# Causal masks and their identity as fp32r in two tables, instead of bf16 in one

## The chip, the cores and the metric

The kernel runs on one core of one Trainium2 chip. The metric is the device time of one launch in microseconds, the median of three runs.

## The reference, cut to what matters

One layer of a decoder: 1024 prompt tokens and 8 decode sequences of 8 tokens, width 1024. One input projection feeds two groups of heads, four differential heads and eight heads of native sparse attention (NSA; two groups of four with shared keys). Their outputs are joined and go through an output projection and a squared-ReLU MLP. Every score that a query must not see is set to -1e9 ahead of the softmax:

```python
def masked_softmax(s, mask):
    s = jnp.where(mask, s.astype(jnp.float32), NEG)
    m = jnp.max(s, axis=-1, keepdims=True)
    p = jnp.where(mask, jnp.exp(s - m), 0.0)
    return p / jnp.maximum(jnp.sum(p, axis=-1, keepdims=True), 1e-30)
# differential heads: kpos[None, :] <= tpos[:, None]
# NSA, compressed keys: cmp_end[None, :] <= tpos[:, None]; its window of 512 has a far edge too
```

The decode tokens attend in the same way to paged caches of 512 past tokens and to the 8 new ones.

## The kernel before, in words

The queries of the prompt are worked off in eight tiles of 128 tokens. Scores are built in PSUM banks of 128x512: two fp32r passes for the two halves of split query values (L404), and then, where a tile crosses the causal diagonal, one more matmul that adds a 128x128 mask of 0 and -1e9 (L411). It has an identity as its weights (`identb`) and the mask (`m_diag`) as its moving data, both bf16. The far edge of the window is added the same way (L408, `m_far`), the compressed branch starts its bank with a mask of 128x256 (L431, `m_cmp`), and the decode scores add masks of 8 columns (L1092 and L1172 `m_new`, L1173 `m_win`). VectorE then reduces the row maximum (L412) and ScalarE takes the exponential (L421).

The masks are loaded by `consts_b` at the start: pieces of the constant `c_mask` come by ScalarE's DMA queue into `raw` tiles and VectorE copies them into `maskb` (L213, L214).

The order of the stages: the projections and keys of NSA; `stage_nsa`, in which the queries of the prompt go through the compressed, selected and window branches (values L496, weights `pt`, values `vst` and `vcp`; the sums of a group are stored to `mixT` at L543); and then `stage_diff`, which works off the differential heads with the decode attention of both kinds beside them. Each decode batch of NSA (`dec_nsa`) loads four cache pages (L1143) and the window state (L1146), each of 128x4x256 fp32 in all, into tiles `kvp` of a pool of five, stores the shifted window back (L1148, L1149), transposes the keys (L1152), scores them (L1167, L1170 and the masks), and, when POOL has scaled the probabilities (L1186, `dpP`), transposes these (L1192). The projection of the differential heads (L331) stands behind that on TensorE. The differential pages are loaded at L1055 and transposed at L1058.

What sets the order: each engine runs its instructions strictly in the order of its own list, and so does each DMA queue (SP issues most of them). The lists come from the framework, which orders the instructions by a simulated schedule. Tiles are allotted from pools that lie one behind the other in SBUF: `xa`, `b`, `sg`, `sm`, then `bn`, which lives until the end of NSA, and then the pools of the stage. When a pool is left, the pools of the next stage take its bytes, and the first instruction that writes a tile waits for the last one that read what lay there:

```python
self.bn = e1(self.pool("bn"))
...
self.kvd = e2(self.pool("kvd", KVB))
...
self.dec_nsa_loads()
self.stage_diff()
```

Of the kernel before, what the change touches and what calls it, by code (L numbers as in the profile page):

```python
# [26 lines left out]
P = 128  # L27
# [3 lines left out]
NT = SEQ // P  # L31
# [15 lines left out]
# schedule  # L47
LAG = 5                  # token tiles by which the first keys / values trail the compression rows
REST = 7                 # items of those left over that go before the compression
QS = 1                   # first query tiles that use a score bank  # L50
KVB = 5                  # page buffers of the decode attention
NSU = (2, 2, 2, 2, 0)    # NSA decode batches around each change of heads
WDN = 10                 # weight buffers of the differential heads
WD = (1, 0, 1)           # per stage: low parts of the weights on VectorE (else GpSimd)
PS_N = (4, 2, 1, 1)      # PSUM banks of scores, transposes, outputs, products: NSA
PS_D = (3, 2, 1, 2)      # the same, differential heads
# [6 lines left out]
def merge(*lists):  # L63
    """emit several lists of (cost, thunk) interleaved in proportion to their total cost"""
# [20 lines left out]
def interleave(*lists):  # L85
    """the items of several lists in the order in which merge would run them"""
    out = []
    merge(*[[(c, lambda i=i: out.append(i)) for i in l for c in [i[0]]] for l in lists])
    return out


class Fill:
    """queue of background work; marks give the point that has to be reached before a given job"""
# [12 lines left out]
    def take(self, budget, key=None):  # L106
        """items up to the mark at least, then up to the budget"""
        need = self.marks.get(key, 0)
        out = []
        c = 0.0  # L110
        while self.pos < len(self.q) and (self.pos < need or c < budget):
            out.append(self.q[self.pos])
            c += self.q[self.pos][0]
            self.pos += 1
        return out
# [5 lines left out]
class Kern:  # L121
# [9 lines left out]
    # ---------------------------------------------------------------- helpers  # L131
# [3 lines left out]
    def evac(self, out, in_, n, scale=None):  # L135
        """PSUM -> SBUF copy on the less loaded of ScalarE and VectorE"""
# [59 lines left out]
    # ---------------------------------------------------------------- setup  # L196
# [7 lines left out]
    def consts_b(self, b):  # L204
        nc, A = self.nc, self.A
        self.identb = b.tile([P, P], BF, name="identb")
        nc.vector.tensor_copy(self.identb, self.ident)
        nm = A["c_mask"].shape[1]
        self.maskb = b.tile([P, nm], BF, name="maskb")
        for c in range(0, nm, 256):  # L210
            n = min(256, nm - c)
            mt = self.rawp.tile([P, 256], F32, name="raw")
            nc.scalar.dma_start(mt[:, :n], A["c_mask"][:, c:c + n])  # L213
            nc.vector.tensor_copy(self.maskb[:, c:c + n], mt[:, :n])  # L214
        self.m_diag = self.maskb[:, 0:128]
        self.m_far = self.maskb[:, 128:256]
        self.m_cmp = self.maskb[:, 256:768].rearrange("p (t n) -> p t n", t=NT)
        self.m_new = self.maskb[:, 768:776]
        self.m_win = self.maskb[:, 776:784]
# [30 lines left out]
    # ---------------------------------------------------------------- phase A: x -> normalised, transposed, split  # L250
    def phase_x(self, px):
        """load a token tile; transpose, split it and take its sum of squares. The weights carry the gain, the
        projections are scaled by 1 / rms on their way out of PSUM"""
# [26 lines left out]
    def gain_cols(self):  # L280
        """g_pre_mix as columns: [128, k]"""
# [7 lines left out]
    # ---------------------------------------------------------------- projections  # L289
    def load_w(self, src, n):  # L290
        """src(k) -> DRAM AP [128, ...] of n columns for contraction block k"""
# [28 lines left out]
    def proj(self, ps, ws, n, t, step=24):  # L320
        """thunks of step products each"""
# [18 lines left out]
    def rope(self, v, t, h):  # L340
        """v: SBUF AP [m, h, 64], rotated in place"""
# [14 lines left out]
    def dup(self, v):  # L356
        """[128, h, 64] -> tile [128, h, 2, 64] with each row block twice"""
# [5 lines left out]
    def k_stack(self, rd, kst, t, T=None):  # L363
        """two doubled sources [128 tok, 128] -> kst[half] [128, 2, 512]; partitions 0-63 hi, 64-127 lo"""
# [10 lines left out]
    def q_stack(self, rd, n, T=None):  # L375
        """n doubled sources [128 tok, 128] -> (hi, lo) stacks [128, n, 128], scaled by 1/8"""
# [10 lines left out]
    # ---------------------------------------------------------------- attention, prompt  # L387
# [3 lines left out]
    def scores(self, qs, j, kst, kc, i, kb0, sums, far):  # L391
        """exp(s - max) for key blocks kb0..i; returns the tile (absolute key columns); sums: [128, 2], one partial
        row sum per 512 keys"""
# [32 lines left out]
    def nsa_cmp_scores(self, g, i, st):  # L426
        """probabilities of the compressed branch, four heads, times gate / sum"""
# [24 lines left out]
    def nsa_scores(self, g, i, pr, st):  # L452
        """thunks: probabilities of heads 2 pr, 2 pr + 1 in the selected and window branches"""
# [30 lines left out]
    def nsa_values(self, g, i, pr, st):  # L484
        """thunks: weighted sums of the values for heads 2 pr, 2 pr + 1, all branches, into st['o']"""
# [64 lines left out]
    def diff_norm(self, od, rows, h, col0):  # L550
        """od: [rows, 128] head output (SBUF) -> sub-layer norm, transpose, store to mixT"""
# [73 lines left out]
    # ---------------------------------------------------------------- compression  # L625
    def unit_cmp(self):
        """projection of the compression branch's k, v rows: one list of thunks per token tile"""
# [32 lines left out]
    def compress_load(self, hb):  # L660
        """thunks: the cached compression rows (keys and values) of four batches, four pages each"""
# [1043 lines left out]
```

## Time and profile before

| | |
|---|---|
| time, median of 3 runs | 1871.66 us (1869.86 to 1874.77) |
| span of the profiled execution | 1873.6 us |
| TensorE busy (PE), weight loads (PEld) | 1783.9 us (95%), 1566.2 us (84%) |
| VectorE, ScalarE, GpSimd | 961.5 us, 720.6 us, 530.2 us |
| L411 masks, PE and PEld | 44.6 us and 18.7 us, 192 each |
| mean granted TensorE clock | 0.976 |

The profiled execution is one more than the three timed ones; its span is 1.9 us above their median and inside their spread, and the profile shows nothing around it. Matmuls are pipelined: the duration of one overlaps with its neighbours, and the time that it takes up is read from the distance of the starts.

### The profile page before, as it was taken

Reading aid. Unit: us, or ns where it says so; the run is one execution under the profiler, and the core shown is the slowest. Engines: PE = TensorE matmul, PEld = TensorE weight load, DVE = VectorE, ACT = ScalarE, POOL = GpSimd, SP = SyncE. Lnnn points to the kernel's source line nnn. Section 1 sums busy time; section 2 is a strip of 40 time slices with the busy share of each in tenths; the row PEclk is TensorE's granted clock in tenths of the full one; section 3 lists DMA queues with packets and bytes.
Section 4 is the critical chain, followed back from the end, with each engine's and each line's share of the span. In section 5 each row is a group of like instructions: output and inputs, shape, how many; then the busy total and the mean of one; then the engine's idle time right before and its main releaser. Section 6 shows DMA issues by size and latency. Waiting matters only on the chain. (4 is left out here: it accounts for less than half of the span.)

```text
span 1873.6 us, 31247 instructions
## 1 busy us (share of the span) xinstructions
PE 1783.9 (95%) x11379; PEld 1566.2 (84%) x11379; DVE 961.5 (51%) x2519; ACT 720.6 (38%) x1987; POOL 530.2 (28%) x749
## 2 busy tenths in 40 slices
PE   6788999999999999999979999999999999999996
PEld 6777776676657788778868799999999999999996
DVE  4357767667754666666564553333333333333336
ACT  4254446556652455555463342222222222222212
POOL 1133325333321111111151023333333333333313
PEclk8899899999999999999989999999999999999998
DMA  8531000022102524324263331111111111111104
GB/s 169 119 86 44 17 12 21 6 80 52 28 8 58 155 72 125 100 66 124 68 201 106 124 119 46 43 43 45 42 45 45 46 46 46 45 46 46 46 1 169
DMA packets 186533, 129.38 MB, mean 69 GB/s; under 512 B 30115, under 2 KB 177419, under 8 KB 186379
## 3 DMA queue, kind: packets, MB, share of 16 engines
q1 hardware_dynamic: 185082, 125.11, 23.5%
q10 hardware_dynamic: 1296, 2.27, 0.5%
q8 instruction: 90, 1.47, 0.3%
q14 instruction: 65, 0.52, 0.1%
HBM read 102.56 MB, written 24.78 MB: 68 GB/s over the span
## 5 line engine op out<-in xcount | busy, mean ns | idle before, releaser
L1355 PE MATMUL Dn<-h,w 128*128 128x384 f32 (+1 forms) x2304 | 388.6, 327 | 2.1 <-DVE w L1401 2.1
L1335 PE MATMUL U<-xt,w 128*128 128x384 f32 (+1 forms) x2304 | 388.5, 326 | 0.2 <-ACT xt L133 0.2
L1355 PEld LDWEIGHTS Dn<-h,w 128*128 128x128 f32 x2304 | 381.8, 188 | 2.3 <-ACT w L1395 2.3
L1335 PEld LDWEIGHTS U<-xt,w 128*128 128x128 f32 x2304 | 380.4, 188 | 0.6 <-ACT xt L133 0.4
L331 PE MATMUL M<-w,xt 128*128 128x384 f32 (+4 forms) x1584 | 294.6, 331 | 13.5 <-ACT nat L133 13.2
L1361 DVE TENSOR_TENSOR acc<-Dn,acc 128x384 f32<-128x384 f32 (+1 forms) x360 | 191.8, 535 | 204.9 <-PE Dn L1355 203.5
L331 PEld LDWEIGHTS M<-w,xt 128*128 128x128 f32 (+1 forms) x1584 | 245.1, 191 | 28.9 <-ACT nat L133 14.7
L162 POOL TENSOR_TENSOR w<-raw,w 128x512 fp32r<-128x512 f32 x128 | 170.8, 1346 | 177.4 <-ACT w L133 177.4
L421 ACT ACTIVATE p<-S,nm 128x512 f32<-128x512 f32 (+3 forms) x288 | 160.1, 562 | 103.6 <-DVE nm L416 57.1
L133 ACT ACTIVATE w<-raw 128x512 fp32r<-128x512 f32 (+1 forms) x160 | 96.6, 609 | 241.8 <-PE U L1335 166.0
L1343 DVE TENSOR_TENSOR h<-r,h 128x384 fp32r<-128x384 f32 (+1 forms) x96 | 52.0, 542 | 261.8 <-POOL r L1342 261.8
L412 DVE TENSOR_REDUCE nm<-S 128x1 f32<-128x512 f32 (+3 forms) x288 | 148.0, 527 | 58.1 <-PE S L411 37.0
L1339 ACT ACTIVATE r<-U 128x384 f32<-128x384 f32 (+1 forms) x96 | 45.4, 473 | 342.3 <-PE U L1335 342.3
L404 PE MATMUL S<-kst,qs 128*128 128x512 f32 (+3 forms) x576 | 163.2, 376 | 9.0 <-ACT p L421 7.9
L1342 POOL TENSOR_TENSOR r<-r 128x384 f32<-128x384 f32 (+1 forms) x96 | 77.3, 805 | 328.6 <-ACT h L1341 328.6
L475 POOL TENSOR_SCALAR p<-p,coef 128x640 f32<-128x640 f32 (+7 forms) x128 | 92.8, 738 | 146.4 <-DVE coef L472 79.6
L404 PEld LDWEIGHTS S<-kst,qs 128*128 128x128 f32 x576 | 94.5, 196 | 21.7 <-ACT p L421 11.1
L169 POOL TENSOR_TENSOR rs_r<-rs_t,mhalf 128x1 f32<-128x1 f32 (+1 forms) x63 | 36.3, 577 | 249.1 <-DVE rs_t L167 236.0
L1267 PE MATMUL C<-w,mh 128*128 128x512 f32 (+1 forms) x432 | 105.5, 401 | 0.8 <-DVE ctmp L1282 0.8
L351 POOL TENSOR_TENSOR rope<-nat,sin 128x128 f32<-128x128 f32 (+3 forms) x81 | 36.3, 448 | 245.5 <-ACT nat L133 234.4
L1267 PEld LDWEIGHTS C<-w,mh 128*128 128x128 f32 (+1 forms) x432 | 78.4, 184 | 22.3 <-DVE ctmp L1282 1.1
L511 PEld LDWEIGHTS T<-ident,p 128*128 128x128 f32 x528 | 57.1, 141 | 39.3 <-issue 35.6
(265 smaller groups left out, 2395.1 us busy)
## 6 DMA issues: line engine op xcount, KB each, us to landing
kvp<-cache_diff_kv SPq DMA_DIRECT2D x128, 128.0 KB
raw<-w_up SPq DMA_DIRECT2D x64, 256.0 KB
raw<-w_down SPq DMA_DIRECT2D x64, 256.0 KB
raw<-w_in SPq DMA_DIRECT2D x32, 192.0 KB
raw<-w_in SPq DMA_DIRECT2D x40, 128.0 KB
xin<-x_prompt SPq DMA_DIRECT2D x8, 512.0 KB
cst<-cache_nsa_kv SPq DMA_DIRECT2D x32, 128.0 KB
kvp<-cache_nsa_kv SPq DMA_DIRECT2D x32, 128.0 KB
```

The lines of the kernel that those rows point to most:

```text
L133: self.nc.scalar.activation(out, in_, AF.Copy, scale=scale)
L162: (nc.vector if self.lo_dve else nc.gpsimd).tensor_sub(lo, raw, f32(hi))
L331: nc.tensor.matmul(ps[1][:m, :n], self.xt[c][:, a, k, c0:c0 + m], ws[k][:, b, :n], start=i == 0, stop=i == len(ops) - 1)
L404: nc.tensor.matmul(S[:, a * P - lo:b * P - lo], qs[:, ps, j, :], kst[hf][:, kc, a * P - lo:b * P - lo], start=ps == 0, stop=ps == 1 and no ...
L412: nc.vector.reduce_max(nm[:, n:n + 1], S[:, a * P - lo:b * P - lo], axis=AX.X, negate=True)
L421: nc.scalar.activation(p[:, a * P:b * P], tiles[n][:, a * P - lo:b * P - lo], AF.Exp, bias=nm[:, 0:1], accum_out=sums[:, n:n + 1])
L475: nc.gpsimd.tensor_scalar(v, v, coef[:, sw + 1, j:j + 1], 0.0, op0=OP.mult, op1=OP.add)
L1267: nc.tensor.matmul(ps[:m], mhs[t][:, a, k, :m], ws[n][k][:, b], start=cnt == 0, stop=cnt == 3 * KC - 1)
L1335: nc.tensor.matmul(U[:, :n], ups[f][k // 4][:, a, k % 4, :], self.xt[c][:, b, k, :], start=cnt == 0, stop=cnt == 3 * KC - 1)
L1342: nc.gpsimd.tensor_mul(r[:, :n], r[:, :n], r[:, :n])
L1355: nc.tensor.matmul(O_[:, :n], dns[dm // 2][:, a, f, (dm % 2) * P:(dm % 2 + 1) * P], hs[f][:, b, :n], start=cnt == 0, stop=cnt == 5)
L1361: nc.vector.tensor_add(acc[c][:, dm], O_[:, :n], acc[c][:, dm])
```

## The change

The identity and the masks become fp32r. The one table of 784 columns in pool `b` is split in two: 144 columns (`m_diag`, `m_new`, `m_win`) stay in `b`, and 640 columns (`m_far`, `m_cmp`) go to `masks` in pool `bn`, which is given back at the end of NSA. The table is loaded in five pieces instead of four, so there is one DMA, one `raw` tile and one copy more. Pool `b` shrinks by 736 bytes per partition, and `bn` grows by 2560. (The rest of the change drops comments.)

```diff
--- before.py
+++ after.py
@@ consts_b
-        self.identb = b.tile([P, P], BF, name="identb")
+        self.identb = b.tile([P, P], FR, name="identb")
         nc.vector.tensor_copy(self.identb, self.ident)
-        nm = A["c_mask"].shape[1]
-        self.maskb = b.tile([P, nm], BF, name="maskb")
-        for c in range(0, nm, 256):
-            n = min(256, nm - c)
+        far = self.bn.tile([P, 640], FR, name="masks")
+        self.maskb = b.tile([P, 144], FR, name="maskb")
+        for c, n, dst in ((0, 128, self.maskb[:, 0:128]), (768, 16, self.maskb[:, 128:144]), (128, 256, far[:, 0:256]),
+                          (384, 256, far[:, 256:512]), (640, 128, far[:, 512:640])):
             mt = self.rawp.tile([P, 256], F32, name="raw")
             nc.scalar.dma_start(mt[:, :n], A["c_mask"][:, c:c + n])
-            nc.vector.tensor_copy(self.maskb[:, c:c + n], mt[:, :n])
+            nc.vector.tensor_copy(dst, mt[:, :n])
         self.m_diag = self.maskb[:, 0:128]
-        self.m_far = self.maskb[:, 128:256]
-        self.m_cmp = self.maskb[:, 256:768].rearrange("p (t n) -> p t n", t=NT)
-        self.m_new = self.maskb[:, 768:776]
-        self.m_win = self.maskb[:, 776:784]
+        self.m_far = far[:, 0:128]
+        self.m_cmp = far[:, 128:640].rearrange("p (t n) -> p t n", t=NT)
+        self.m_new = self.maskb[:, 128:136]
+        self.m_win = self.maskb[:, 136:144]
```

In the list of TensorE all separate weight loads of the bf16 identity go: 192 at L411, 32 at L408, 16 at L431 and 8 each at L1092, L1172 and L1173, 264 in all; the fp32r matmul loads its weights itself, as those of L404 do. The matmuls stay 10580. In the changed list the mask matmuls of L411 and L408 stand right ahead of an L331 in 46 places, of an L404 of 256 columns or more in 57 and of 128 columns in 13, of an L496 in 41, and of a transpose or another fp32 matmul in 67.

In the differential stage the page buffers `kvp` begin 736 bytes lower (170464 in place of 171200), and in the NSA stage the values of the second group, `vst`, end 1824 bytes higher (172064 in place of 170240). So the first page buffer now lies on `vst`.

SP's list at the change from NSA to the differential heads, before: the first pages (`cache_nsa_kv`) and the window states stand among the stores of `mixT`, in front of 13 loads of `w_in`, and the loads wait (in brackets, a counter of the DMA queue or of an engine) for PE alone.

```order
L543 DMA mixT<-pt 64x4x128 [waits DMAHW3_49,DVE_49]
L1143 ISA
L1143 DMA kvp<-cache_nsa_kv 128x256 [waits DMAHW4_49,PE_49]
L1143 ISA
L1143 DMA kvp<-cache_nsa_kv 128x256 [waits DMAHW5_49]
L1143 ISA
L1143 DMA kvp<-cache_nsa_kv 128x256 [waits DMAHW6_49]
L1143 ISA
L1143 DMA kvp<-cache_nsa_kv 128x256 [waits DMAHW7_49]
L1146 DMA kvp<-state_nsa_win_kv 128x4x256 [waits DMAHW0_49,PE_49]
```

The same loads in the changed kernel:

```order
L960 DMA o_diff_s<-nat 128x1x128 [waits DMAHW3_49,DVE_49,Activation_49]
L1143 ISA
L1143 DMA kvp<-cache_nsa_kv 128x256 [waits DMAHW4_49,PE_49,Pool_49]
L1143 ISA
L1143 DMA kvp<-cache_nsa_kv 128x256 [waits DMAHW5_49]
L1143 ISA
L1143 DMA kvp<-cache_nsa_kv 128x256 [waits DMAHW6_49]
L1143 ISA
L1143 DMA kvp<-cache_nsa_kv 128x256 [waits DMAHW7_49]
L543 DMA mixT<-pt 64x4x128 [waits DMAHW0_49,DVE_49]
L1146 DMA kvp<-state_nsa_win_kv 128x4x256 [waits DMAHW1_49]
```

They now stand behind the loads of `w_in`, behind the store of `o_diff_s` and behind all stores of `mixT` but the last, and the PE instruction for which the first page waits is the last L496 on `vst` of the NSA stage. The last store of `mixT`, which is the fold of the second group, stands between the pages and the window.

TensorE's list at the same place, before: the last values of NSA, the transposes of the first batch's pages and window and its first scores.

```order
L496 MATMUL o<-pt,vst 64x256 [waits Activation_49]
L496 MATMUL o<-pt,vcp_1467 64x256 [waits DVE_49]
L1152 MATMUL T<-ident,kvp 128x128 [waits DMAHW4_49,PE_49]
L1152 MATMUL T<-ident,kvp 128x128 [waits DMAHW5_49]
L1152 MATMUL T<-ident,kvp 128x128 [waits DMAHW6_49]
L1152 MATMUL T<-ident,kvp 128x128 [waits DMAHW7_49]
L1152 MATMUL T<-ident,kvp 128x128 [waits DMAHW0_49,PE_49]
L1152 MATMUL T<-ident,kvp 128x128 x3
L1167 MATMUL S<-kt,qndec 64x260 [waits Activation_49]
```

The same place in the changed kernel:

```order
L496 MATMUL o<-pt,vst 64x256 [waits Activation_49]
L496 MATMUL o<-pt,vcp_1471 64x256 [waits DVE_49]
L1152 MATMUL T<-ident,kvp 128x128 [waits DMAHW4_49,PE_49]
L1152 MATMUL T<-ident,kvp 128x128 [waits DMAHW5_49]
L1152 MATMUL T<-ident,kvp 128x128 [waits DMAHW6_49]
L1152 MATMUL T<-ident,kvp 128x128 [waits DMAHW7_49]
L1167 MATMUL S<-kt,qndec 64x260 [waits Activation_49]
L1167 MATMUL S<-kt,qndec 64x260 [waits DVE_49]
L1152 MATMUL T<-ident,kvp 128x128 [waits DMAHW1_49]
L1152 MATMUL T<-ident,kvp 128x128 x3
```

The end of the values and the first transposes stand next to each other in both. In the changed list the load of the pages is released by the last L496 on `vst`, and between it and the transposes that read these pages only the product on `vcp` is left. Behind these rows the window of the first batch, the pages and then the window of the second follow, then L1192, and only then the first L331 of the projection.

## Rows read from the trace of the kernel before

**Rows 1.** The page: span, then busy time of each engine.

```profile
span 1873.6 us, 31247 instructions
PE 1783.9 (95%) x11379; PEld 1566.2 (84%) x11379; DVE 961.5 (51%) x2519; ACT 720.6 (38%) x1987; POOL 530.2 (28%) x749
```

**Rows 2.** All mask instructions of L411: min/median/max ns, first and last start.

```profile
L411 PEld LDWEIGHTS <-identb x192: 95/96/146, 178.9 to 970.3; 128*128 128x128 bf16 x192
L411 PE MATMUL S<-maskb,identb x192: 218/230/330, 178.9 to 970.3; 128*128 128x128 bf16 x192
```

**Rows 3.** Groups by line: busy us, mean ns, idle before, releasers.

```profile
L404 PEld LDWEIGHTS S<-kst,qs 128*128 128x128 f32 x576 | 94.5, 196 | 21.7 <-ACT p L421 11.1 <-issue 4.7 <-ACT qs L133 2.2
```

**Rows 4.** Timeline of PE, four places: start us, us, instruction.

```profile
72.31 3.00 PE L331 MATMUL M<-w,xt 128*128 128x256 f32 x24
75.15 0.38 PE L370 MATMUL T<-ident,rd 128*128 128x128 f32 x2
...
228.21 0.23 PE L411 MATMUL S<-maskb,identb 128*128 128x128 bf16 x1
228.25 0.84 PE L331 MATMUL M<-w,xt 128*128 128x256 f32 x5
228.93 0.34 PE L404 MATMUL S<-kst,qs 128*128 128x384 f32 x1
...
330.35 0.23 PE L411 MATMUL S<-maskb,identb 128*128 128x128 bf16 x1
330.42 0.50 PE L511 MATMUL T<-ident,p 128*128 128x128 f32 x3
...
448.36 0.23 PE L411 MATMUL S<-maskb,identb 128*128 128x128 bf16 x1
448.40 0.71 PE L404 MATMUL S<-kst,qs 128*128 128x512 f32 x2
448.95 0.23 PE L411 MATMUL S<-maskb,identb 128*128 128x128 bf16 x1
```

**Rows 5.** Timeline of the start: the last copy of a mask on VectorE.

```profile
27.21 0.17 DVE L214 CAST maskb<-raw 128x16 bf16<-128x16 f32 x1 [3.09 <-DMA raw<-c_mask]
```

**Rows 6.** Timeline of SP in NSA: the first page loads.

```profile
381.87 2.35 SPq L1143 DMA_DIRECT2D kvp<-cache_nsa_kv  x4
...
384.91 1.93 SPq L1143 DMA_DIRECT2D kvp<-cache_nsa_kv  x4
```

**Rows 7.** Timeline of all engines at the change from NSA to the differential heads.

```profile
558.64 0.65 PE L496 MATMUL o<-pt,vst 128*64 128x256 f32 x2
...
559.86 1.09 PE L1152 MATMUL T<-ident,kvp 128*128 128x128 f32 x8
...
561.45 0.58 SPq L543 DMA_DIRECT2D mixT<-pt  x1
...
564.62 0.18 PE L1172 MATMUL S<-maskb,identb 128*128 128x8 bf16 x1
...
569.07 0.66 PE L1192 MATMUL T<-ident,dpP 128*128 128x128 f32 x4 [1.23 <-POOL dpP L1186]
...
570.22 4.89 PE L331 MATMUL M<-w,xt 128*128 128x384 f32 x19
```

**Rows 8.** Timeline of SP later: a window load and the store that waits for it, twice.

```profile
639.20 0.39 SPq L1146 DMA_DIRECT2D kvp<-state_nsa_win_kv  x1
...
646.85 0.37 SPq L1148 DMA_DIRECT2D o_win_s<-kvp  x1
...
841.80 0.56 SPq L1146 DMA_DIRECT2D kvp<-state_nsa_win_kv  x1
...
846.08 0.38 SPq L1148 DMA_DIRECT2D o_win_s<-kvp  x1
```

**Rows 9.** Windows: us, busy time (instructions) of each engine, granted clock, DMA share, GB/s.

```profile
568.00:572.00 4.00, 2.93 (x14) 2.59 (x15) 1.79 (x10) 1.63 (x7) 0.70 (x1) 0.71 0.00 0
572.00:576.00 4.00, 4.00 (x24) 3.93 (x24) 0.63 (x4) 0.58 (x4) 0.70 (x1) 0.86 0.00 0
```

## The prediction

> **What bounds the kernel now.** The page comes first: PE is busy for 1783.9 of 1873.6 us and, its own weight loads aside, no other engine for more than 51% [rows 1]. So the time is that of PE's list, and a change costs or gives what it does to the distances of PE's starts. Two things on that list are touched: each mask matmul, and the place where PE goes from NSA to the differential heads. For the masks I read the instructions of their line [rows 2], the weight loads of the score matmuls beside them [rows 3] and PE's timeline around single masks [rows 4]; the reader is to take the distance from one start to the next there, not the duration. For the change of stages I read SP's queue where the pages are loaded [rows 6] and the timeline of all engines where they are used [rows 7]: between the two lie 175 us.
>
> **The change part by part: the masks.** In an fp32r stream 24 matmuls of 256 columns take from 72.31 to 75.15, which is 0.118 us each [rows 4]. An fp32r mask of 128 columns loads the same 128x128 weights and should cost about that, so 0.118 us is my price for the new one, wherever it stands. The old one is read by what follows it:
>
> - Ahead of an L331 (46 places): the mask at 228.21 is followed by five L331 and the next start is at 228.93, 0.72 us later. Five L331 are 0.59, so the mask held PE for 0.13. The change gives 0.012 x 46 = 0.55 us.
> - Ahead of a wide L404 (57): from 448.36 to 448.95 a mask and two L404 of 512 columns take 0.59. [...]
> - Ahead of a transpose or other fp32 work (67): 330.35 to 330.42, so 0.07. The new one costs 0.048 more, x 67 = 3.2 us.
> - Ahead of an L404 of 128 columns (13): I take the same loss, 0.6 us. Ahead of an L496 (41): no row isolates it, and it lies between the gain at L331 and the loss at transposes; I take nothing.
>
> The sum is -0.55 - 1.7 + 3.2 + 0.6 = +1.6 us. [...] The bf16 weight loads that vanish are 96 ns each [rows 2], and run beside a matmul; they are inside the distances above and are not taken off once more.
>
> **The load of the masks.** One DMA of 64 KB, one buffer and one copy are added. The last copy now ends at 27.4, after a wait of 3.09 for its DMA [rows 5]; the first L411 is at 178.9 [rows 2]. So masks that come a few us later are needed 150 us after that: 0. What else is moved is that ScalarE's queue issues one DMA more, and that the weights share the four `raw` buffers; nothing in the rows prices that, and I allow -2 to +2.
>
> **The change of stages.** This is the larger term. Before, the pages of the first two decode batches are issued at 381.87 and 384.91 [rows 6], and PE transposes them at 559.86 [rows 7]. They were hidden behind all of the second group's NSA. In the changed kernel the first page buffer lies on `vst`, so the load waits for the last L496 on `vst`. That one runs from 558.64 to 559.29 [rows 7]. Everything that SP has behind this load waits too: four pages, the window, four more pages, the second window, 2 MB in all. The steps, on the clock of before:
>
> - 559.4: four pages issue, 1.93 us as at 384.91 [rows 6], until 561.4. The last store of `mixT` follows; its fold is as before, so it issues at 561.45 for 0.58 [rows 7].
> - 562.1: the first window issues. Of two other windows the store that waits for the landing starts 4.28 us (841.80) and 7.65 us (639.20) after the issue [rows 8]; in the second case other transfers stood between. I take 4.3: landed at 566.4.
> - From there PE still has the second half of the first batch. Before, 16 transposes and their scores took 4.76 us, 559.86 to 564.62 [rows 7]. With half of the transposes left I take half, 2.4: L1172 at 568.8.
> - From L1172 to L1192 the softmax runs through VectorE, ScalarE and POOL, 564.62 to 569.07, 4.45 us, and PE waits for POOL at its end [rows 7]. So L1192 is at 573.2 and L331, 1.15 us behind it, at 574.4. It was at 570.22: **+4.2 us**.
> - The second window issues at 564.7 behind its pages (1.93 more) and lands at 569.0 by 4.3. Its scores take to 571.4, and so are hidden behind the softmax of the first batch. By 7.65 it lands at 572.4, its scores end at 574.8, and L331 starts at 575.9: +5.7.
>
> Below: if half the softmax is hidden behind the second batch's work and the windows land in some 3 us, 2 us remain. Above: both windows at 7.65, +7.5. The 19 L331 and what follows have their data, and are merely late. The differential pages (L1055) move behind these loads; their first use comes after the L331 block of 4.89 us [rows 7], which covers them if they land in the few us that the windows take. Without that cover, up to 2 us more.
>
> [...]
>
> **Sum.** +1.6 + 4.2 = +5.8 us. The profiled execution's span, 1873.6, would become 1879.4; it stands 1.9 us above the median of the three runs, within their spread of 4.9, so I put the sum on the median: 1871.66 + 5.8 = **1877.5 us**. About 0.3%, 5.6 us, is what a measurement of this kernel can tell from no change; the forecast lies at that edge.
>
> **The rivals.**
> [...]
> - *The loads are hidden anyway* (about 1873). SP could reach them before the release and PE's other work could fill the gap, so that only +1.6 stays, 1873.3. Against: PE runs in the order of its list, and nothing but the product on `vcp` stands there between release and use.
> [...]
> - *The weight load is exposed* (about 1899). The load of fp32r weights at L404 takes 196 ns [rows 3], that of the bf16 identity 96 [rows 2]. If the 100 ns of difference stood on the path at each of 224 masks, it would be +22.4 with the stages' 4.2: 1898. Against: L331 has a load for every matmul too, and its starts are 0.118 apart [rows 4], with the load beside the matmul ahead of it. [...]
>
> **How the numbers follow.** The forecast gets 0.56, its own range 1874 to 1882; longer loads 0.15; hidden loads 0.13; the other side 0.11; exposed weight loads 0.05. From the forecast half lies above the 5.6 us, half below. Slower by over 0.3%: 0.28 + 0.15 + 0.05 and 0.01 of the hidden loads = 0.49. Within 0.3%: 0.28 + 0.12 + 0.01 = 0.41. Faster: 0.10. The range from 1868 to 1886 leaves out the exposed weight loads and most of the other side.
>
> **What the profile of the changed kernel would show.** No bf16 load at L411, and masks about 0.12 us from the next start, ahead of transposes too; if the distance there stays at 0.07 or goes to 0.2, the masks' term is wrong. The first L1143 would be issued right behind the last L496 on `vst`, a few tenths of a us after it; PE would wait at L1152 for the pages and again for the window, and the first L331 behind L1192 would be some 15 us after that L496, not 11. If L1143 stands early and PE's waits there are as before, the stage's term is wrong. The forecast fails altogether if PE's list, reordered at many places, gains or loses waits elsewhere; the sum has no term for that.

## The result

Before: 1872.16 us (median of 4 runs, 1869.86 to 1874.77). After: 1893.78 us (4 runs, 1889.86 to 1900.54). The ratio is 1.0122, 95% interval 1.0097 to 1.0147: slower by some 22 us, where 1877.5 with a range of 1868 to 1886 was forecast. Timed once more later on, the changed kernel took 1892.99, ratio 1.0115 (1.0097 to 1.0133).

The head of the page of the changed kernel, which answers to [rows 1]:

```profile
span 1891.7 us, 31245 instructions
PE 1794.0 (95%) x11379; PEld 1592.4 (84%) x11379; DVE 964.9 (51%) x2520; ACT 721.0 (38%) x1987; POOL 531.6 (28%) x749
```

PE is as full as before, and its matmuls are as many; the weight loads grew by 26 us. All mask instructions of L411 in the changed kernel, beside [rows 2]:

```profile
L411 PEld LDWEIGHTS S<-maskb,identb x192: 187/188/334, 179.8 to 986.5; 128*128 128x128 f32 x192
L411 PE MATMUL S<-maskb,identb x192: 218/223/415, 179.9 to 986.9; 128*128 128x128 f32 x192
```

A load of the fp32r identity takes 188 ns, of the bf16 one 96; the matmul itself has kept its length (median 223 ns, 230 before). Whether the load costs PE anything, this view can't say.

PE's timeline at the change of stages in the changed kernel, beside [rows 7]:

```profile
564.50 0.65 PE L496 MATMUL o<-pt,vst 128*64 128x256 f32 x2
565.15 0.64 PE L496 MATMUL o<-pt,vcp 64*64 64x256 f32 x2
567.77 0.61 PE L1152 MATMUL T<-ident,kvp 128*128 128x128 f32 x2 [1.97 <-DMA kvp<-cache_nsa_kv]
...
570.70 1.99 PE L1167 MATMUL S<-kt,qndec 128*64 128x260 f32 x4 [1.14 <-ACT kt L133]
572.62 1.97 PE L1152 MATMUL T<-ident,kvp 128*128 128x128 f32 x8
...
576.45 0.38 PE L1172 MATMUL S<-maskb,identb 128*128 128x8 f32 x1
...
580.91 0.66 PE L1192 MATMUL T<-ident,dpP 128*128 128x128 f32 x4 [0.54 <-POOL dpP L1186]
...
581.90 1.30 PE L331 MATMUL M<-w,xt 128*128 128x384 f32 x6
```

And SP's queue there, beside [rows 6] and [rows 8]:

```profile
565.30 1.98 SPq L1143 DMA_DIRECT2D kvp<-cache_nsa_kv  x4
567.39 0.59 SPq L543 DMA_DIRECT2D mixT<-pt  x1
568.03 0.60 SPq L1146 DMA_DIRECT2D kvp<-state_nsa_win_kv  x1
...
570.83 0.43 SPq L1146 DMA_DIRECT2D kvp<-state_nsa_win_kv  x1
572.55 0.38 SPq L1148 DMA_DIRECT2D o_win_s<-kvp  x1
...
576.38 0.35 SPq L1148 DMA_DIRECT2D o_win_s<-kvp  x1
```

The last values on `vst` end at 565.15 and the pages are issued at 565.30. PE waits 1.97 us for them, and the first L331 starts 16.75 us after those values, where it was 10.9 before [rows 7]. The clock fell inside this stretch. Windows of the changed kernel, columns as in [rows 9]:

```profile
568.00:572.00 4.00, 2.34 (x7) 1.16 (x7) 0.24 (x2) 0.60 (x1) 0.00 (x0) 0.77 0.82 237
572.00:576.00 4.00, 4.00 (x16) 2.30 (x14) 0.84 (x3) 0.60 (x1) 0.00 (x0) 0.50 1.06 347
576.00:580.00 4.00, 3.34 (x19) 1.87 (x17) 2.65 (x11) 1.40 (x6) 0.00 (x0) 0.88 0.81 237
...
584.00:588.00 4.00, 4.00 (x30) 3.73 (x28) 0.63 (x4) 0.42 (x2) 0.70 (x1) 1.00 0.04 12
```

From 572 to 576 the granted clock was 0.50; behind the stall, where [rows 9] show 0.71 and 0.86, it is 1.00.

**Where along the list the time went.** All kernels here but the one with doubled masks have the same number of matmuls on PE, so the start of the n-th matmul can be compared between two traces. The table gives how many us later than in the second profile of the kernel before (b1 below) the matmul starts that b1 starts at the time in the head; each start is counted from the beginning of its own span, and the labels are those of the experiments below. The first row, another profile of the same kernel, shows what one execution differs from another: up to 7 us on the way.

```
b1 starts it at (us)           134   221   512   594   786  1075  1245
before, first profile          2.0   2.0   2.0   2.5   6.7   5.5   5.4
after                          2.0   5.6   7.8  12.3  14.7  22.4  23.5
after, again (ra)              5.0   8.4  10.5  15.3  20.2  24.3  24.3
fp32r, own order (r3)          5.0   7.4   6.1   6.4   8.3  13.9  13.5
bf16 in e3's order (e8)       -2.6   0.6   0.6   0.7   2.6   7.4   7.6
fp32r, order of before (r7)    7.7   7.4   7.5   7.7  10.1  10.0  10.6
bf16, the same lists (r9)      7.4   7.9   7.8   8.0   9.5   8.6   8.6
bf16, new layout (e1)          5.3   5.9   5.8  12.4  15.1  12.9  12.8
before + 1824 bytes (e4)       5.8   5.9   5.8  12.3  17.4  15.0  14.8
before, 32 bytes off (y3)      7.0   7.1   6.9   7.0  10.0   7.0   6.8
before, masks late (x4)        5.9   4.5   6.1   4.5   3.6  -3.1  -3.2
```

In the changed kernel's two profiles the change of stages (512 to 594) cost 4.5 and 4.8. The larger part is elsewhere: 134 to 221, 221 to 512, and 594 to 1075.

### The profile page after: what moved, and what is told of

It is laid out like the page before. It is cut to its first block, busy times and chain, and to the rows that moved or that the text cites. A ratio compares the mean times of both kernels' runs of the same rounds, so it can differ in the third digit from the quotient of the medians.

```text
span 1891.7 us, 31245 instructions
## 1 busy us (share of the span) xinstructions
PE 1794.0 (95%) x11379; PEld 1592.4 (84%) x11379; DVE 964.9 (51%) x2520; ACT 721.0 (38%) x1987; POOL 531.6 (28%) x749
## 5 line engine op out<-in xcount | busy, mean ns | idle before, releaser
L331 PE MATMUL M<-w,xt 128*128 128x384 f32 (+4 forms) x1584 | 290.2, 328 | 17.8 <-ACT nat L133 15.1
L331 PEld LDWEIGHTS M<-w,xt 128*128 128x128 f32 (+1 forms) x1584 | 243.5, 190 | 31.4 <-ACT nat L133 16.6
L404 PE MATMUL S<-kst,qs 128*128 128x512 f32 (+3 forms) x576 | 165.1, 376 | 10.7 <-ACT p L421 10.3
L404 PEld LDWEIGHTS S<-kst,qs 128*128 128x128 f32 x576 | 94.4, 197 | 24.6 <-ACT p L421 13.7
L1267 PEld LDWEIGHTS C<-w,mh 128*128 128x128 f32 (+1 forms) x432 | 78.9, 185 | 22.4 <-DVE ctmp L1282 1.1
```

Source lines behind the costliest of these rows:

```text
L331: nc.tensor.matmul(ps[1][:m, :n], self.xt[c][:, a, k, c0:c0 + m], ws[k][:, b, :n], start=i == 0, stop=i == len(ops) - 1)
L404: nc.tensor.matmul(S[:, a * P - lo:b * P - lo], qs[:, ps, j, :], kst[hf][:, kc, a * P - lo:b * P - lo], start=ps == 0, stop=ps == 1 and no ...
L1267: nc.tensor.matmul(ps[:m], mhs[t][:, a, k, :m], ws[n][k][:, b], start=cnt == 0, stop=cnt == 3 * KC - 1)
```

## The experiments

The theories: *late pages* (the loads of L1143 wait for the end of `vst`), *type* (a price at each fp32r mask), *lists* (the changed types make the framework order all engines anew, and the new order costs), *load* (five pieces of masks instead of four), and, from the results on, *addresses* (the tiles behind the masks' pools begin elsewhere). Times are medians, with the ratio to the kernel before on the same chip and its 95% interval.

**e1: bf16 in the new layout.** The tiles keep the bytes of the changed kernel, so the layout and the five loads stay and the type goes.

```diff
-        self.identb = b.tile([P, P], FR, name="identb")
+        self.identb = b.tile([P, 2 * P], BF, name="identb")[:, 0:P]
-        far = self.bn.tile([P, 640], FR, name="masks")
-        self.maskb = b.tile([P, 144], FR, name="maskb")
+        far = self.bn.tile([P, 1280], BF, name="masks")
+        self.maskb = b.tile([P, 288], BF, name="maskb")
```

> The changed kernel with its two tables and its identity in bf16 again, in tiles of the same bytes, so that every pool lies where it does in the changed kernel and the first page buffer lies on the values. The time before was about 1872, of the changed kernel about 1893. If the late page loads are the larger cause, this stays near the changed kernel: 1884 to 1894. If the fp32r masks are, it falls back to within 8 us of the kernel before (the stall of 4 to 6 us stays): 1876 to 1880. If the reshuffled lists are the cause, it lands anywhere from 1872 to 1895, and its losses stand at other places than those of the changed kernel.

1878.66, 1.0029 (1.0013 to 1.0046): +5.4 us by the ratio. The layout costs that, with the order that the framework gives this kernel (its list of PE differs from that of before at 232 of 11379 places, the changed kernel's at 778); the rest of the loss, some 17 us, needs the type, by itself or by the order that comes with it. (The execution in the table was this kernel's longest, 1883.28.)

**e4: the kernel before, with `bn` longer by 1824 bytes** that nothing uses, so that the page buffers lie on `vst`.

```diff
+                    self.bn.tile([P, 456], F32, name="padn")
```

> The kernel before with an unused tile of 1824 bytes in the pool that lives until the end of NSA, so that the end of the values reaches over the first page buffer. Masks, tables and their loads are untouched. Late loads as the larger cause: 1880 to 1890, with PE waiting at L1152 and the first L331 behind L1192 some 15 us or more after the last values. Masks as the cause: 1876 to 1879. Lists: between 1872 and 1895.

1882.3, 1.0044 (1.0027 to 1.0061). PE's timeline of e4 at the change of stages:

```profile
562.53 0.65 PE L496 MATMUL o<-pt,vst 128*64 128x256 f32 x2
...
565.91 0.30 PE L1152 MATMUL T<-ident,kvp 128*128 128x128 f32 x1 [2.09 <-DMA kvp<-cache_nsa_kv]
...
579.27 0.66 PE L1192 MATMUL T<-ident,dpP 128*128 128x128 f32 x4 [1.38 <-POOL dpP L1186]
```

The wait for the pages is there without any change of the masks, and the step in the table from 512 to 594 is 6.5. Late pages stand as a mechanism, and come from the bytes alone. But e4 was 5.8 late at 134 us already, where no page is near; that was unexplained at this point.

**e3: fp32r with the page buffers beside the values.** A tile of 1280 bytes ahead of `kvd` keeps the pages off `vst`. `m_far` and `m_cmp` stay bf16 with an identity of their own, so 216 of the 264 masks are fp32r.

```diff
-        far = self.bn.tile([P, 640], FR, name="masks")
+        far = self.bn.tile([P, 640], BF, name="masks"); self.identf = self.bn.tile([P, P], BF, name="identf"); nc.vector.tensor_copy(self.identf, self.ident)
...
+                    self.padp = e2(self.pool("padp"))
+                    self.padp.tile([P, 320], F32, name="padt")
```

> The masks of the diagonal and of the decode scores in fp32r as in the changed kernel (216 of 264); the far edge and the compressed branch keep a bf16 table and a bf16 identity; 1280 unused bytes ahead of the page buffers, so that these lie beside the values. Late loads as the larger cause: the loads are issued near 382 again, no wait at L1152, and 1870 to 1877. Masks as the cause: 1882 to 1890. Lists: anywhere from 1872 to 1890, with losses elsewhere.

1886.09, 1.0059 (1.0038 to 1.008). The pages are early again, as SP's queue in e3 shows, its step from 512 to 594 is 0.2, and 11 us stay. So late pages are the smaller part.

```profile
385.09 1.96 SPq L1143 DMA_DIRECT2D kvp<-cache_nsa_kv  x4
```

**e6: each mask of L411 added twice** to the changed kernel, 192 fp32r masks more (the scores behind the mask change, since -2e9 is added).

```diff
+                nc.tensor.matmul(S[:, i * P - lo:(i + 1) * P - lo], self.identb, self.m_diag, start=False, stop=False)
                 nc.tensor.matmul(S[:, i * P - lo:(i + 1) * P - lo], self.identb, self.m_diag, start=False, stop=True)
```

> The changed kernel with every mask of the diagonal (192) added twice, which changes no result since the exponential of -2e9 is 0 as well. It prices one fp32r mask: by the start distances in the trace of the changed kernel (0.06 us to the next start) 192 times 0.06 to 0.118 is 12 to 23 us, so 1905 to 1916 (late loads, lists). If a mask costs what the masks theory needs, 16 us over 224 masks more than the bf16 one, so some 0.2 us each, 192 of them give 38 us, 1931.

1918.6, 1.0235 (1.0198 to 1.0272), a little above the 1905 to 1916 that was expected. That is 24.8 us above the changed kernel by the medians and 21 by the ratios, so 0.11 to 0.13 us for each mask. A mask more costs about what the prediction took for a mask; but the lists of e6 were ordered anew as well, so it doesn't price the type.

**e7, e8 and e9: the lists held.** The order in which every engine runs its instructions was recorded (but for the few that set up the masks and the constants) and given to another kernel by order-only edges between neighbours in each list, which add no wait on a semaphore. e7 is e3 in the order of before; e8 is the kernel before in the order of e3; e9 is e7 with the 216 masks bf16 again in tiles of the same bytes.

```diff
+            tc.add_manual_dep(i, prev.name, mybir.DependencyInfo(mybir.DependencyClass.NoSync, mybir.DependencyReason.DATA),
+                              reason="recorded order")
```

> The kernel with 216 fp32r masks and the page buffers beside the values (the one that measured about 11 us over the kernel before), with the list of PE, VectorE and ScalarE held instruction for instruction in the order of the kernel before, GpSimd's and SP's to a few instructions. Only the type of the masks and the addresses differ from the kernel before. If the reshuffled lists are what the masks cost, the 11 us go: 1872 to 1876. If the fp32r masks themselves cost it, 1881 to 1887 stays.

> The kernel before, bf16 masks and one table, with the lists of that kernel of 216 fp32r masks, held instruction for instruction on PE, VectorE and ScalarE. Lists as the cause: 1880 to 1887, with PE waiting for VectorE's query copy (L383) near 193 us as there. Type of the masks as the cause: 1870 to 1876.

> The kernel of 216 fp32r masks held in the order of the kernel before, with these masks and their identity in bf16 again, in tiles of the same bytes. All five engines' lists are the same instruction for instruction as there, and so are the addresses and the five loads of the masks; only the type of the mask matmuls differs. That one measured about 9.7 us over the kernel before. If the type costs it: 1869 to 1874. If what is left (five loads instead of four, one more copy and identity, a slightly other start of the lists, other addresses) costs it: 1877 to 1883.

e7 1880.06, 1.0052 (1.0036 to 1.0068), between the two times that were expected and so no answer by itself. e8 1879.51, 1.0057 (1.0035 to 1.008): bf16 masks, no late page, the old addresses, and some 10 us lost by the order alone, just under the 1880 to 1887 that was expected of the lists. e9 1877.38, 1.0017 (1.0004 to 1.0029). Since e9 ran on another chip than e7, the pair could not be compared closely, and it was run again.

**The kernel before against itself.** 

> The kernel before itself, unchanged, timed against itself: a second profile of it, and how far two kernels that are the same come apart in this comparison. Ratio within 0.15% of 1; in the profile the start phase up to 120 us and the end of the differential stage from 950 to 1000 us differ from the first profile by some us, the rest by less than one, if it is these two that vary from run to run.

1870.88, 0.9987 (0.9975 to 0.9999). So a single ratio can be off by 0.1%.

**r9, r7, r3 and ra: e9, e7, e3 and the changed kernel unedited, on one chip** (before: 1870.34).

> Second timing of the bf16 kernel of the same lists. If what both share (five loads, an identity and a copy more, the first lines of the lists, addresses) costs the time: 3 to 8 us over the kernel before, like its fp32r twin. If not: within 2 us of the kernel before.

> Second timing of the kernel with 216 fp32r masks in the order of the kernel before, beside the one with bf16 masks in the same lists, on one chip, since their two ratios (1.0052 and 1.0017) came from different calls while their two traces, matched matmul by matmul, differ by 2 us and by nothing at the masks of 128 columns. If the type of the masks costs time: 5 us or more above the bf16 one again. If it doesn't: within 3 us of it.

> Second timing of the 216 fp32r masks in the order that the scheduler gives them. If the reshuffled lists cost time: 3 us or more above its twin in the order of the kernel before. If they don't: within 2 us of it.

> The changed kernel again, beside these. It has the reshuffled lists of the third and the late page loads. If lists, start and loads add: 4 to 8 us above the third, so 15 to 23 above the kernel before. In its second profile the step at the change of stages is 4 to 6 us again, and the losses in the start, at 600 to 900 us and at the end of the differential stage are other ones if they are a matter of the clock's windows, the same ones if they are a matter of the lists.

r9 1877.02, 1.0036 (1.0024 to 1.0047); r7 1877.59, 1.0040 (1.0025 to 1.0054); r3 1885.38, 1.0077 (1.006 to 1.0094); ra 1892.99, 1.0115 (1.0097 to 1.0133). Step by step, each as the difference of two ratios on 1870.3: same lists and bf16, but other addresses and five loads, +6.7 us; the type, +0.7; the new order, +6.9; late pages, the rest of the masks and their order, +7.1. The uncertainty of the first step is 2 us, of each other one 3 to 5.

How little the type matters is seen in PE's timeline of r9 (bf16) and r7 (fp32r), whose lists are the same. First r9, then r7:

```profile
454.18 0.23 PE L411 MATMUL S<-maskb,identb 128*128 128x128 bf16 x1
454.22 0.71 PE L404 MATMUL S<-kst,qs 128*128 128x512 f32 x2
454.77 0.23 PE L411 MATMUL S<-maskb,identb 128*128 128x128 bf16 x1
```

```profile
453.72 0.22 PE L411 MATMUL S<-maskb,identb 128*128 128x128 f32 x1
453.78 0.68 PE L404 MATMUL S<-kst,qs 128*128 128x512 f32 x2
454.30 0.22 PE L411 MATMUL S<-maskb,identb 128*128 128x128 f32 x1
```

From mask to mask it is 0.59 and 0.58. The next start comes 0.02 later behind an fp32r mask, and the two L404 take 0.03 less. Over all pairs of the two traces, from the matmul ahead of a mask to the second one behind it, the fp32r mask changes the distance by a median of -0.013 us ahead of L331, -0.012 ahead of L404, -0.011 ahead of L496 and -0.004 ahead of transposes; the 24 masks of 8 columns cost 0.092 more each. Together about +0.4 us (-0.013 x 41 - 0.012 x 52 - 0.011 x 36 - 0.004 x 63 + 0.092 x 24). So the type costs 0.4 us where it acts, and 0.7 by the times, within their 3.5. (The profiled executions of r7 and r9 end 2.0 us apart, more than the places of the masks account for.)

The lists: VectorE in the changed kernel and, in the next fence, in b1, near the first queries; the third fence is PE in the changed kernel, the fourth PE in b1.

```profile
190.20 0.23 DVE L889 TENSOR_SCALAR gates<-M,rx 128x24 f32<-128x24 f32 x1
...
191.73 2.15 DVE L773 RECIPROCAL p<-p 128x160 f32<-128x160 f32 x2
...
193.97 0.62 DVE L383 SCALAR_TENSOR_TENSOR qs<-M,qs 128x512 fp32r<-128x512 f32 x1
```

```profile
187.06 0.23 DVE L889 TENSOR_SCALAR gates<-M,rx 128x24 f32<-128x24 f32 x1
...
189.89 0.69 DVE L383 SCALAR_TENSOR_TENSOR qs<-M,qs 128x512 fp32r<-128x512 f32 x1 [0.16 <-ACT qs L133]
...
190.85 2.16 DVE L773 RECIPROCAL p<-p 128x160 f32<-128x160 f32 x2
```

```profile
194.64 1.71 PE L435 MATMUL S<-kcst,qs 128*128 128x64 f32 x7 [2.35 <-DVE qs L383]
```

```profile
190.64 1.71 PE L435 MATMUL S<-kcst,qs 128*128 128x64 f32 x7 [0.30 <-DVE qs L383]
```

The new order puts two reciprocals ahead of the copy of the queries. From L889 to L383 it is 3.77 us instead of 2.83, and PE, which needs the copy, waits 2.35 instead of 0.30 (the wait alone is not the measure: in r7, in the order of before, it is 1.29, and the four L380 ahead of it took 0.66 us there, 1.11 in b1). In the table r3, e8 and both profiles of the changed kernel lose 2.4 to 3.6 us from 134 to 221; r7, r9, e1, e4 and y3 lose -0.3 to 0.6. Of that, 1.6 to 2.0 us come between the matmuls that b1 starts at 188 and at 194, which is this place, in every trace of a new order (these four, e3 and y1), and 0.0 to 0.3 in the ten traces in the order of before.

The other place is the stage of the differential heads. Windows from 600 to 1080 us of the changed kernel, of r3 and of e8 (columns as in [rows 9]):

```profile
600.00:1080.00 480.00, 455.71 (x2937) 379.45 (x2936) 291.63 (x833) 235.04 (x681) 99.11 (x177) 0.96 0.37 111
```

```profile
600.00:1080.00 480.00, 454.44 (x2941) 378.46 (x2938) 293.99 (x835) 238.15 (x688) 100.86 (x176) 0.98 0.36 110
```

```profile
600.00:1080.00 480.00, 455.68 (x2944) 373.25 (x2943) 291.56 (x824) 237.02 (x682) 100.34 (x173) 0.97 0.37 112
```

And of r7 and r9, and of b1 (PE's busy time, granted clock, DMA share and GB/s alone), in the order of before:

```profile
600.00:1080.00 480.00, 457.60 (x2968) 378.36 (x2969) 296.77 (x841) 239.89 (x692) 97.39 (x176) 0.98 0.37 111
```

```profile
600.00:1080.00 480.00, 459.51 (x2976) 374.43 (x2975) 297.21 (x841) 240.19 (x692) 97.46 (x176) 0.98 0.37 112
```

```profile
600.00:1080.00 480.00, 458.30 (x2976) 0.98 0.38 115
```

In the new order PE idles 24.3 to 25.6 us of these 480 and gets through 2937 to 2944 matmuls; in the old one 20.5 to 22.4, and 2968 to 2976. In the table from 594 to 1075 the kernels in a new order lose 6.7 to 10.1 us, those in the order of before or near it (the first profile, r7, r9, e1, e4, y3) 0.0 to 3.0; x4, in an order of its own, gains 7.6.

The idle time is less than half of that. The rest is the granted clock: 0.96 to 0.98 looks alike, but 0.01 of 480 us is 4.8 us. Taken over the same matmuls, from the one that b1 starts at 594 to the one at 1075, the six traces of a new order (the four above, e3 and y1) idle 25.0 us in the mean, and the clock that wasn't granted comes to 14.8 us of full speed; in the ten in the order of before it is 21.9 and 10.4. Single traces overlap in both (24.0 to 25.7 against 20.4 to 24.0; 11.9 to 17.1 against 5.1 to 13.7). So the new order costs about 3 us by waits and about 4 by a lower clock here; what brings the clock down was not tested. One place stands out: between the matmuls that b1 starts at 934 and 954 the new order loses 1.0 to 3.8 us and the old one -0.7 to 0.9, and PE waits there for ScalarE's `pt` (L608) for 1.5 to 2.3 us in the new order and 1.1 at most in the old.

**x1, x2 and x4: the load.** x1 is the kernel before with five loads, its lists held. x2 is e9 with four loads, the first of which is copied into both tables. x4 is the kernel before with the masks' loads written behind those of the first keys.

```diff
-        for c in range(0, nm, 256):
-            n = min(256, nm - c)
+        for c, n in ((0, 128), (768, 16), (128, 256), (384, 256), (640, 128)):
```

> The kernel before, bf16 and one table, which loads the masks in the five pieces of the changed kernel instead of four, with PE's, VectorE's and ScalarE's lists held as before. If the fifth load (one buffer more of the four that the weights need in the start, one issue and one copy more) costs the 6.7 us that the kernels of the same lists lost: 1875 to 1879, with the loss ahead of 130 us. If the addresses and the second table do: 1868 to 1873.

> The bf16 kernel of the same lists and two tables, with four loads as before (one of them is copied into both tables). Fifth load as the cause: back to 1868 to 1873. Addresses and the second table: it stays at 1875 to 1879.

> The kernel before with the four loads of the masks traced behind the projections of the first keys instead of ahead of them; its lists are its own. If buffers of the weights are what the loads cost in the start, it may gain 2 to 5 us there: 1865 to 1871; if its other lists cost more than that, 1871 to 1880.

x1 1872.1, 1.0003 (0.9994 to 1.0013). x2 1877.37, 1.0032 (1.0021 to 1.0043). x4 1870.35, 0.9999 (0.9987 to 1.0012). The fifth load costs nothing, and taking it away gives nothing. The place of the loads is not priced by x4, since its lists are its own: in the table it is late at 134 us and makes up for it from 594 on. It does show that an order other than that of before (317 of PE's places differ) need not cost anything. What x2 has left against the kernel before, with the order held, is where its tiles lie.

**y3, y2 and y1: the addresses.** `cst` receives the cached rows for the compression, 128 KB at a DMA, while the kernel starts. It begins at byte 108800 of a partition in the kernel before (425 x 256), at 109600 in x2, r7 and r9 and at 110624 in the changed kernel, both 32 bytes past a multiple of 256. The pads stand in `sm` and move every tile behind it, not `cst` alone; but of the tiles that DMA fills between 20 and 70 us (`cst`, `xin`, `raw`) only `cst` lies there, since the others are allotted from the other side (`side="right"`). y3 moves it in the kernel before by 32 bytes; y2 moves it in x2 by 224, to 429 x 256; y1 moves it in the changed kernel by 32, to 110656, a multiple of 64 but not of 256. The lists are those of the kernel that was padded.

```diff
-                self.sm = e(self.pool("sm"))
+                self.sm = e(self.pool("sm")); self.sm.tile([P, 8], F32, name="pad32")
```

> The kernel before with 32 unused bytes ahead of the pools whose tiles receive the cache pages and the compression rows: `cst` from 108800 to 108832, `kvp` from 171200 to 171232. All lists are the same, instruction for instruction. In the profiles so far, the kernels with `cst` at a multiple of 64 bytes moved 145 to 150 GB/s between 20 and 70 us, one with it 32 bytes off 135 at the same DMA share, with packets of 1 KB taking 87 to 92 ns in place of 75 to 82. If the address is the cause of the shared loss of 5 to 7 us: 1876 to 1880, with the loss ahead of 130 us. If it isn't: 1870 to 1874.

> The bf16 kernel of two tables and four loads, in the lists of the kernel before (1.0032 of its time), with 224 unused bytes, so that `cst` is at a multiple of 256 again (109824), as in the kernel before, and `kvp` at one of 64. Address as the cause: 1870 to 1874. Otherwise it stays at 1875 to 1879.

> The changed kernel with 32 unused bytes: `cst` at 110656 (a multiple of 64, not of 256), `kvp` at 170496 (a multiple of 256, and still on the values). The lists are those of the changed kernel. If 64 bytes are what matters: 5 to 7 us less than the changed kernel, 1884 to 1889. If 256 are: the start stays slow, 1888 to 1894.

y3 1875.77, 1.0019 (1.0007 to 1.0032). y2 1872.18, 1.0006 (0.9995 to 1.0017). y1 1889.09, 1.0094 (1.0081 to 1.0108). The windows from 20 to 70 us (columns as in [rows 9]) of x1 and y2, whose `cst` is at a multiple of 256:

```profile
20.00:70.00 50.00, 33.18 (x242) 30.64 (x243) 18.56 (x61) 18.52 (x38) 7.77 (x23) 0.93 0.80 150
```

```profile
20.00:70.00 50.00, 34.51 (x229) 31.99 (x229) 17.62 (x59) 16.98 (x35) 7.20 (x20) 0.86 0.80 147
```

Of x2 and y3, where it is 32 bytes past one:

```profile
20.00:70.00 50.00, 31.82 (x190) 28.89 (x190) 15.53 (x52) 14.54 (x30) 6.06 (x17) 0.83 0.81 135
```

```profile
20.00:70.00 50.00, 31.04 (x196) 28.64 (x197) 16.90 (x56) 16.62 (x35) 6.65 (x19) 0.83 0.80 142
```

The DMA engines are as busy, 0.80 and 0.81, and move less (the two profiles of the kernel before moved 151 and 145 GB/s), and PE gets through 190 or 196 matmuls instead of 229 or 242. The first masks say the same later: L411 in these four starts first at 178.3 and 178.3, against 187.9 and 184.0, all in the same lists. The 1824 bytes of e4 put its `cst` at 110624 too, which fits its 5.8 us at 134. So 32 bytes cost the kernel before 0.19%, 3.6 us, just under the 1876 to 1880 that was expected, and the 224 bytes more give x2 all of its loss back but 0.06%, both against the kernel before on their own chip.

y1 is not as clear. Its time is 0.2% better than ra's on another chip, with intervals that overlap, and at 134 us its profile is 4.1 late, where the two of the changed kernel are 2.0 and 5.0. 1889.09 lies where the two ranges that were expected meet, and decides nothing.

## Why the prediction was wrong

**Which step failed.** Two. The first is the sum itself, which had "no term" for "PE's list, reordered at many places". The new order cost +6.9 us timed from r7 to r3 (within 4), some 10 from the kernel before to e8, and it is the largest item in the changed kernel's own profiles: 3.4 and 3.6 us from 134 to 221, 2.1 and 2.2 from there to 512 (r3 and e8 lose nothing there, and no run holds the changed kernel's own order apart) and 9.0 and 10.1 from 594 to 1075, of which the kernels in the old order lose 0.0 to 3.0 too. The prediction named this as the way in which it would fail, without a price. The second is "The load of the masks", "0", with -2 to +2. The five loads did cost 0 (x1). But moving the tiles behind them made the start slower, +6.7 us in r9 and +3.6 in y3, outside those bounds. The changed kernel itself is 2.0 and 5.0 late at 134 us, so less of it may act there.

**The change of stages held.** By its own steps: the pages issued 0.15 us after the last values on `vst`; the window landed, as its store shows, 7.4 us after them (572.55), where 7.1 was reckoned; L1172 came 3.9 behind that, not 2.4, with a granted clock of 0.50 from 572 to 576; from L1172 to L1192 it took 4.46, where 4.45 was read from before; and L331 came 0.99 behind that, not 1.15. Together 16.75 instead of 15.1. Since the low granted clock that stood behind the stall before (0.71 and 0.86 [rows 9]) has moved into it (0.77, 0.50 and 0.88 from 568 to 580, 1.00 after that), the list as a whole lost 4.5 and 4.8 us there, and 4.2 was forecast. The bf16 kernels with the same overlap, e1 and e4, lose 6.6 and 6.5. The second wait that the prediction named, at L1152 for the window, didn't show: the window had landed by 572.55, and PE came to it at 572.62.

**The masks.** The term was +1.6; the pair r7 and r9 gives +0.7 by the times, within 3.5 us, and about +0.4 by the traces. The price of 0.118 us for an fp32r mask was wrong as "wherever it stands": a mask of 128 columns between two wide L404 held PE for 0.06 before the next start, and 0.07 ahead of transposes was not raised to 0.118 (-0.004 from r9 to r7). The gain of 0.012 ahead of L331 was right. What costs are the 24 masks of 8 columns, 0.092 us each. That the result comes near the +1.6 is partly luck. No run shows the 1.7 us that the sum takes off for the masks ahead of wide L404: between r9 and r7 the gain there is 0.012 at each of 52, 0.6 together. The loss of 3.2 ahead of transposes isn't there, and the 2.2 of the short masks was not in the sum.

**The rivals.** Longer loads: no, the windows landed in 4.5 and 5.55 us (568.03 to 572.55, 570.83 to 576.38), where [rows 8] had 4.28 and 7.65. Hidden loads: no, PE waited 1.97 us for the pages. The other side, a faster kernel: no, the gain at a mask of 128 columns is 0.013 us at most, and the new order lost time, +6.9 us from r7 to r3. The exposed weight load: no. The 1898 that it gave lies close to the time that came, but r7 has 92 ns more at each of its loads of L411 (188 against 96 ns) and is 0.7 us from r9. The cost of the longer load doesn't show: an fp32r mask starts 0.06 us ahead of the next matmul (453.72 and 453.78 in r7), so most of a load of 188 ns runs beside other matmuls.

**What stays open.** The terms do not add up to better than some 5 us: e1 and e4 have both the moved `cst` and the late pages, and cost 5.4 and 8.2 us, where 6.7 and 4.5 would make 11.2. How much of the moved `cst` acts in the changed kernel's own order is not settled, nor which single exchange of neighbours costs what between 594 and 1075, nor what brings the clock down there; one place, near 195 us, was shown. No run had the changed kernel's full set of masks in the order of before, and none of the kernels tried was faster than the kernel before.

## What to carry to other kernels

A change of types or tile sizes, where a framework orders the lists and packs the pools, changes three things beside the work itself: the order on every engine (which cost some 10 us in e8 and came out even, 0.9999, in x4), which tile lies on which (6.5 us at the change of stages in e4), and the address of every tile behind it (3.6 us in y3). Look at all three before pricing the instruction, and hold the order (a recorded list, order-only edges) to price the instruction at all. Where a prefetch must stay early, check which bytes its buffer shares, and with whose last reader.

## What the runs showed of the hardware that was not expected

The loads of `cst` were slower when their destination in SBUF started 32 bytes past a multiple of 256. With lists held, packets of 1 KB in the first 120 us took a mean of 79.8 and 82.1 ns in the kernel before, 81.6 in x1 and 78.9 in y2, but 89.6 in y3, 92.2 in x2, 89.6 in r9 and 91.4 in r7: some 12% more, where the DMA engines are busy for 0.80 of the time (20 to 70 us). The packets of 4 KB, whose tiles the pads don't move, took as long in y3 (244 ns) as in the kernel before (249 and 241). Orders of their own fall on the same sides: 74.5 in e8 and 82.8 in x4, at a multiple of 256, and 85.2 to 90.9 in e1, e3, e4, e6 and r3, 32 bytes past one. The changed kernel is less plain: 84.5 and 89.4 in its two profiles, and 84.8 in y1, at a multiple of 64. Whether 64 bytes would do is open, and no run moved `cst` alone.

A weight load that is twice as long (188 against 96 ns) cost nothing that shows at the masks of 128 columns (-0.013 to -0.004 us each between r9 and r7). A mask of 8 columns cost 0.092 us more as fp32r; why it does was not tested.
